# Whole runs of small TensorE tiles in a one-layer hybrid decoder step, with a planner that charges changes of tile shape

## The chip, the core and the metric

The kernel runs on one core of one Trainium2 chip. The metric is the device time of one execution in microseconds (us), as a median over runs. TensorE (PE in the profile) does the matrix products, VectorE (DVE) and ScalarE (ACT) the elementwise work, GpSimd (POOL) a little copying, and the queue of SyncE (SP) issues all DMAs. Each engine executes its own instructions in the order in which they stand in the program, and waits on semaphores for the others.

## What is computed

One layer of a decoder step, for a prompt of 512 tokens and for 8 samples of 4 tokens each. All tokens go through one input projection; branch A is dilated sliding-window attention with 3 groups of 8 heads, branch B a gated delta rule in chunks with 8 heads of 128; both are merged, projected and normed.

```python
h = x * (1 + scale[:, None]) + shift[:, None]
qa, ka, va, za, qkv_b, zb, a_b, b_b, ga, gb = split_columns(h @ w_in)       # 1024 x 11280
# branch A, for each group (window, dilation) in ((128,1),(512,4),(2048,16))
logits = einsum('bqhd,bqjhd->bqhj', q, k_sel) * 64 ** -0.5 + bias
p = exp(logits - max); s = sum(p); out = einsum('bqhj,bqjhd->bqhd', p / s, v_sel); lse = m + log(s)
o_a = combine over groups with softmax(lse)
# branch B, for each chunk
lower = where(strict, beta * kk * decay, 0) + eye(n)
sol = triangular_solve(lower, concat([beta * v, beta * k * exp(cum)]))       # u, w
v_new = u - w @ state; out = (q * exp(cum)) @ state + (qk * decay) @ v_new
state = exp(cum[-1]) * state + (k * tail).T @ v_new
# back
merged = sigmoid(ga) * ((o_a * silu(za)) @ w_branch_a) + sigmoid(gb) * ((norm(o_b) * silu(zb)) @ w_branch_b)
y = LayerNorm(ALPHA * x + gate * (merged @ w_out))
```

## The kernel before

**The stream.** The 544 token columns (512 prompt, 32 sample) stand in two halves of 272. The projection is cut into 88 jobs of one 128-column tile of `w_in` each. A job is 48 matmuls: for each half and each of 8 pieces of the contraction, three products of rounded halves (`hhi,hi`, `hhi,lo`, `hlo,hi`, all fp32r, 128x272) are summed into one PSUM bank `pp`, of which there are two. ScalarE and VectorE split each weight tile into `hi` and `lo` and empty the banks. Jobs of the branch outputs (`ybh`, `yah`) and the last product (`wo`) have the same manner. These matmuls fill TensorE wherever nothing else is ready.

**Side work.** Beside the stream run, as generators: the delta rule (`delta_blocks`, `delta_rule`, one head after the other), the prompt attention (`prompt_attention`, four head pairs j), and the samples. In the profile's names `pg<-k,q` is a score product of the prompt attention, `pg<-PT,vrow` a product with the values, `pg<-cst,P` a transpose between them, `pg<-cst,st` the transposes of the softmax sums at the end of two pairs, `pd<-Tc,NTs`, `pd<-W,Xc`, `pd<-XF,W`, `pd<-W,XF`, `pd<-U,NTs` and `pd<-XF,U` the stages of the triangular inverse, and `pd<-vn,kr`, `pd<-vn,QKd`, `pd<-S,KQ`, `pd<-z,XF` the steps of the delta rule over its four chunks.

**Shapes and positions.** A product whose contraction or whose output rows are under 128 uses a part of the TensorE array only: a score product takes 64 rows by 128 columns of it, a value product 128 by 64, an inverse stage 32 by 32 or 64 by 64. Score products of the two heads of a pair (`hh`) lie at array rows 0 and 64 and write two different banks; value products of the two heads lie at array columns 0 and 64 and write one bank `pn`. In the code the two heads alternate already. The 16 steps (j, i) of the attention have 6 score products each (two of them 256 columns wide where i is not 0) and 8 value products (6 where i is 0). Three PSUM banks (`pg`) serve scores, transposes and value sums together.

**The order.** Nothing is issued as it is written. A `Recorder` (line 245) notes every operation; `schedule` (line 419) then plays all engines on costs of its own (`cost`, line 335) and at each point gives an engine the ready operation of least rank (the stream has rank 9, the attention 3). The order that comes out is emitted for each engine. On PE it keeps two kinds apart, fp32r (`rounded`) and the rest: while fp32r is running, others that have been ready for less than `HOLD` = 1 us are kept back (line 551), and a change between the kinds is charged 0.054 or 0.097 us (line 576). Operations recorded under `together()` (line 328) form a group that is issued without another instruction of that engine between them. Before the change that is used for the sample values, the gate rows and a loop on VectorE, not for scores, prompt values or inverse stages. A new PSUM tile is given out when its first operation is a candidate.

**The end of the prompt attention.** After the last `st` transposes of the pairs j = 2 and 3 come VectorE's work on the weights `R` and `Z`, four DMAs `dw<-R` to device memory, eight DMAs `wv<-dw` back, and VectorE's products of `ya` and `NB` with them. The SBUF pools of that phase are then closed and those of the next opened, in which the first `zt` tile of the jobs `zb` lies. Two halves of a job can go to the two `pp` banks before that; the next half has to wait until `zt` has emptied one.

**The caches.** 168 DMAs of 512 KB (`out_kv_s<-in_cache`) copy the caches from device memory to device memory. Each has an earliest time in the planner's clock (48 to 850 us, evenly), so that they lie between the other DMAs of SP's queue.

Of the kernel before, what the change touches and what calls it, by code (L numbers as in the profile page):

```python
# [12 lines left out]
F32R = mybir.dt.float32r  # L13
# [230 lines left out]
class Recorder:  # L244
# [4 lines left out]
    OVER = {"ve": 0.08, "se": 0.10, "ge": 0.05}  # L249
    AGAIN = {"pe": 0.0, "ve": 0.11, "se": 0.14, "ge": 0.11, "sp": 0.0}  # L250
    HOLD = 1.0
    ENGINES = ("pe", "ve", "se", "ge", "sp")
    FREE = ("g", "d", "b")

# [72 lines left out]
    @contextmanager  # L327
    def together(self):

        self.group = []  # L330
        yield
        self.group = None


    def cost(self, op, args):
        size = lambda v: math.prod(v.shape[1:])
        views = op.outs + op.ins
        n = max([size(v) for v in views] or [1])
# [4 lines left out]
        op.transfer = None  # L343
        e = "sp" if op.name == "dma_start" else op.engine
        if e == "pe":
            op.rounded = False
            if op.name == "transpose":
                c = 0.117
            else:
                m, n = size(args[1]), size(args[2])  # L350
                op.rounded = args[1].dtype == F32R
                if op.rounded:
                    c = 0.455 * n + 2
                elif m > 64:
                    c = max(200, 1.93 * n + 5)
                elif m > 32:
                    c = max(120, 1.21 * n)
                else:
                    c = max(18, 0.57 * n)
                c /= 1000  # L360
            op.cost, op.late = c, 0.165
        elif e == "ve":
            if op.name == "reciprocal":
                c = 0.15 + 6.25e-3 * n
            elif op.name == "memset":
                c = 0.06 + 0.83e-3 * n
# [52 lines left out]
    def schedule(self):  # L419
# [33 lines left out]
        parked_pool, lanes, rounded = {}, {}, [True]  # L453
        busy, cold, held = [], {}, {}
        push, pop = heapq.heappush, heapq.heappop

        def candidate(op):
# [22 lines left out]
            for d, data in op.deps.items():  # L480
                p = ops[d]
                if p.engine != op.engine or p.transfer is not None:
                    r = max(r, p.done + self.WAKE[op.engine] + self.margin(p, op) if data else p.end)
                else:
                    r = max(r, p.end + (self.AGAIN[op.engine] if data else 0.0))
            for t in op.tiles:
# [30 lines left out]
        while done < len(ops):  # L517
# [28 lines left out]
            elif not avail[e]:  # L546
                free[e] = t
                continue
            else:
                op = None  # L550
                if e == "pe" and rounded[0] and not avail[e][0][-1].rounded:

                    if t - min(x[-1].ready for x in avail[e] if not x[-1].rounded) < self.HOLD:
                        x = min((x for x in avail[e] if x[-1].rounded), default=None)
# [153 lines left out]
def body(ctx, tc, io):  # L708
# [517 lines left out]
    def delta_rule(h):  # L1226
# [13 lines left out]
        for c in range(4):  # L1240
            for a in range(0, 128, 32):
                pe.matmul(pwv[a:a + 32, c, :], NTs[a:a + 32, c, a:a + 32], Tc[a:a + 32, c, 0:16],
                          start=True, stop=True, tile_position=(a, a))
# [4 lines left out]
        for c in range(4):  # L1248
            for a in range(0, 128, 32):
                pe.matmul(pxv[a:a + 32, c, :], Xc[a:a + 32, c, :], W0[a:a + 32, c, :],  # L1250
                          start=True, stop=True, tile_position=(a, a))
# [10 lines left out]
        for c in range(4):  # L1262
            for a in (0, 64):
                pe.matmul(pwv[a + 32:a + 64, c, :], NTs[a:a + 32, c, a + 32:a + 64], Tc[a:a + 32, c, :],
                          start=True, stop=True, tile_position=(a, a + 32))
# [5 lines left out]
        for c in range(4):  # L1271
            for a in (0, 64):
                x22 = XF[a + 32:a + 64, c, a + 32:a + 64]
                w = W[a + 32:a + 64, c, :]
                if a == 0:
                    pe.matmul(pxv[32:64, c, :], x22, w, start=True, stop=True, tile_position=(32, 32))
                pe.matmul(pxv[a:a + 32, c, :], w, x22, start=True, stop=True, tile_position=(a + 32, a))
# [4 lines left out]

        pw = pd()
        pwv = pw[:, 0:256].rearrange("p (s m) -> p s m", m=64)
        for c in range(4):
            pe.matmul(pwv[64:128, c, :], NTs[0:64, c, 64:128], U[0:64, c, :],
                      start=True, stop=True, tile_position=(0, 64))
# [4 lines left out]
        for c in range(4):  # L1292
            pe.matmul(pxv[0:64, c, :], U[64:128, c, :], XF[64:128, c, 64:128], start=True, stop=True,
                      tile_position=(64, 0))
        ve.tensor_scalar(XF[0:64, :, 64:128], pxv[0:64], -1.0, None, op0=OP.mult)
        yield 1.7

# [86 lines left out]
    def prompt_attention():  # L1384

        for j in range(4):
# [28 lines left out]
            def scores(i):  # L1415
# [1 line left out]
                tk = slice(128 * i, 128 * i + 128)  # L1417
                k0 = 0 if i else 128
                pS = [pg(), pg()]
                for g in range(3):  # L1420
                    for hh in range(2):
                        hp = slice(64 * hh, 64 * hh + 64)
                        if g == 0:
                            pe.matmul(pS[hh][:, k0:256], qt[0][hp, tk], kt[0][hp, 128 * (i - 1) + k0:128 * (i + 1)],
                                              start=True, stop=True)
                        else:
                            pe.matmul(pS[hh][:, 128 + 128 * g:256 + 128 * g], qt[g][hp, tk], kt[g][hp, tk],
                                      start=True, stop=True)
                Ps = []
                for hh in range(2):  # L1430
                    h4 = 2 * (j % 2) + hh
# [11 lines left out]
            for i in range(4):  # L1443
# [12 lines left out]
                    PTs.append(PT)  # L1456
                    yield 1.2 + 0.5 * hh

                for c in range(c0_, 4):
                    for hh in range(2):  # L1460
                        hp = slice(64 * hh, 64 * hh + 64)
                        g = max(c - 1, 0)
                        v = vrow[g][:, i - 1 if c == 0 else i, hp]
                        pe.matmul(pnv[hp, c > 1, i % 2, :], v, PTs[hh][:, c, :], start=c in (c0_, 2), stop=c in (1, 3))
# [812 lines left out]
```

## Time and profile before

| what | us |
|---|---|
| median of 3 runs (971.05 to 979.1) | 971.42 |
| span of the profiled execution, first to last instruction | 969.5 |
| PE busy / weight loads busy | 915.4 / 837.9 |
| DVE busy | 739.3 |
| ACT busy / POOL busy | 416.1 / 78.8 |

The profiled execution has no other time of its own than its span, which lies 1.9 us below the median; that difference holds what lies around the first and the last instruction, and the spread of the runs. All matmuls of one fp32 product (not of fp32r) stand as two records each, a product being done in two passes; a transpose is one record. Records of PE overlap, since matmuls are pipelined: the busy time of a group counts overlaps once, and the distance from one start to the next is what a matmul costs the stream. All operations carry the line of the helper that emits them (L655 before, L670 after), so groups are told apart by their tiles.

### The profile page before, as it was taken

The numbers are of one execution on the slowest core, as the hardware profiler recorded it, in microseconds if no ns is written. First come the engines' busy times: TensorE is split into PE (matmuls) and PEld (weight loads), VectorE is DVE, ScalarE is ACT, GpSimd is POOL, SyncE is SP. The second block draws the span as 40 slices with busy tenths as digits, with TensorE's granted clock in tenths as the row PEclk, the third lists the DMA queues.
The fourth block names the chain that finished last, engine by engine and source line by source line (L and its number), as shares of the span: only waits on it lengthen the run. The fifth ranks groups of instructions, "written<-read, shape, count | busy, mean of one in ns | idle before, by whom it ended". The sixth has DMA issues, their size and how long they took to land.

```text
span 969.5 us, 20678 instructions
## 1 busy us (share of the span) xinstructions
PE 915.4 (94%) x8070; PEld 837.9 (86%) x8070; DVE 739.3 (76%) x1620; ACT 416.1 (43%) x973; POOL 78.8 (8%) x176
## 2 busy tenths in 40 slices
PE   4899999999999999999999799998999999999895
PEld 1599988999988998889998698897998999997785
DVE  0575556866899999699989867556899899847658
ACT  0365347553657553457453546341532222234421
POOL 0110001100010300012402100002020000000000
PEclk9799999999999999999999799999999999999998
DMA  9677855676977697968787746559879999975513
GB/s 357 211 229 232 235 178 208 218 198 185 306 260 251 189 296 245 322 218 277 263 280 257 256 140 210 167 179 314 296 253 338 365 416 374 316 256 169 192 38 113
DMA packets 106340, 237.76 MB, mean 245 GB/s; under 512 B 30898, under 2 KB 62140, under 8 KB 103556
## 3 DMA queue, kind: packets, MB, share of 16 engines
q1 hardware_dynamic: 106244, 236.45, 72.7%
q8 instruction: 63, 1.03, 0.4%
q14 instruction: 33, 0.27, 0.1%
HBM read 220.40 MB, written 103.70 MB: 334 GB/s over the span
## 4 chain that ended last, share of the span: by engine, by line
PE 65%; DVE 18%; DMA 10%; issue 3%; ACT 2%; SPq 2%; POOL 0%; DVEq 0%; ACTq 0%; POOLq 0%
PE pp L655 48%; PE pg L655 9%; PE pd L655 5%; PE pb L655 3%; DVE lo L655 2%; DVE r L655 2%; DVE slab L655 2%; DMA wc<-in_w_cond 2%; DVE acc L655 2%; SPq L655 2%; DMA wv<-dw 1%; DMA out_kv_s<-in_cache 1%; DVE tmp L655 1%; DVE Tb L655 1%; DMA S<-in_state_delta 1%
## 5 line engine op out<-in xcount | busy, mean ns | idle before, releaser
L655 PE MATMUL pp<-hhi,hi 128*128 128x272 f32 x1408 | 414.5, 295 | 9.2 <-DVE zt L655 2.6
L655 PE MATMUL pp<-hhi,lo 128*128 128x272 f32 x1408 | 414.6, 295 | 0.0
L655 PE MATMUL pp<-hlo,hi 128*128 128x272 f32 x1408 | 411.9, 293 | 0.5 <-DVE hlo L655 0.5
L655 PEld LDWEIGHTS pp<-hhi,hi 128*128 128x128 f32 x1408 | 267.9, 190 | 12.9 <-DVE zt L655 3.0
L655 PEld LDWEIGHTS pp<-hlo,hi 128*128 128x128 f32 x1408 | 268.0, 190 | 3.1 <-issue 1.0
L655 PEld LDWEIGHTS pp<-hhi,lo 128*128 128x128 f32 x1408 | 267.5, 190 | 3.2 <-issue 2.2
L655 ACT ACTIVATE hi<-wt 128x1024 fp32r<-128x1024 f32 (+1 forms) x104 | 106.7, 1026 | 184.0 <-PE pp L655 148.7
L655 DVE TENSOR_TENSOR lo<-wt,hi 128x1024 fp32r<-128x1024 f32 (+1 forms) x104 | 122.6, 1179 | 58.1 <-ACT hi L655 55.5
L655 DVE SCALAR_TENSOR_TENSOR acc<-ext,cw,acc 128x568 f32<-128x568 f32 x72 | 57.5, 799 | 0.9 <-ACT acc L655 0.4
L655 ACT ACT_TABLE_LOAD x36 | 46.2, 1283 | 13.9 <-DMA cT<-in_cT 8.2
L655 DVE TENSOR_TENSOR slab<-slab 128x512 f32<-128x512 f32 (+1 forms) x66 | 42.8, 665 | 7.4 <-DMA slab<-in_vs 3.0
L655 ACT ACTIVATE P<-P,st 128x256 f32<-128x256 f32 (+1 forms) x64 | 31.3, 490 | 28.4 <-DVE st L655 27.9
L655 DVE TENSOR_REDUCE slab<-slab 128x8 f32<-128x512 f32 (+2 forms) x66 | 42.6, 655 | 0.3
L655 POOL COPY cx<-ext 128x3 f32<-128x3 f32 (+1 forms) x48 | 33.7, 732 | 75.2 <-ACT ext L655 75.0
L655 PE MATMUL pp<-ybh,hi 128*128 128x272 f32 x128 | 37.2, 290 | 1.3 <-ACT zt L655 1.3
L655 PE MATMUL pp<-ybl,hi 128*128 128x272 f32 x128 | 36.9, 289 | 0.0
L655 PE MATMUL pp<-ybh,lo 128*128 128x272 f32 x128 | 36.9, 288 | 0.0
L655 ACT ACTIVATE zt<-pp 128x272 f32<-128x272 f32 x48 | 18.5, 388 | 31.5 <-PE pp L655 31.5
L655 PE MATMUL pg<-k,q 64*128 64x128 f32 (+1 forms) x192 | 30.5, 329 | 0.0
L655 DVE CUSTOM_DVE_ANT_0 P<-pg,bias 128x256 f32<-128x256 f32 (+1 forms) x64 | 24.3, 402 | 6.2 <-PE pg L655 5.6
L655 ACT ACTIVATE ext<-pp 128x272 f32<-128x272 f32 (+2 forms) x72 | 20.0, 315 | 19.8 <-PE pp L655 16.4
L655 ACT ACTIVATE spare<-pp 128x272 f32<-128x272 f32 (+1 forms) x32 | 16.1, 503 | 26.0 <-PE pp L655 25.9
(395 smaller groups left out, 1587.0 us busy)
## 6 DMA issues: line engine op xcount, KB each, us to landing
out_kv_s<-in_cache SPq DMA_DIRECT2D x144, 512.0 KB
wt<-in_w_in SPq DMA_DIRECT2D x88, 512.0 KB
out_kv_s<-in_cache SPq DMA_DIRECT2D x24, 496.0 KB
wc<-in_w_cond SPq DMA_DIRECT2D x8, 1024.0 KB
slab<-in_ks SPq DMA_DIRECT2D x32, 256.0 KB
slab<-in_vs SPq DMA_DIRECT2D x32, 256.0 KB
kv<-in_ks SPq DMA_DIRECT2D x16, 512.0 KB
kv<-in_vs SPq DMA_DIRECT2D x16, 512.0 KB
```

Source lines behind the costliest of these rows:

```text
L655: getattr(real[x.engine], x.name)(*map(arg, x.args), **{k: arg(v) for k, v in x.kw.items()})
```

## The change

There are four parts. Six loops of the inverse stages, the score products and the value products are put under `together()`, with the operations unchanged. In a group each operation now depends in order on the one before it, and the first operation takes on all tiles of the group, so that the group begins only when all its banks are free and all its inputs are there. The planner's PE costs are changed: each product has a shape (`form`: rows and columns of the array, each 32, 64 or 128) and a `place` in it; a change of shape waits for all places and is charged `TURN` = 0.092 us; within a shape smaller than the whole array a product holds its own place for its cost and PE for `ISSUE` = 0.016 us; the costs are new (a transpose 0.111 for 0.117, an fp32 product with more than 64 output rows at least 0.222 us for 0.2, at 1.75 for 1.93 ns a column). And `HOLD` is kept per shape: while one shape is running, operations of another that have been ready for under 1 us are kept back.

```diff
         self.ops.append(op)
         if op.group is not None:
+            if op.group:
+                op.deps.setdefault(op.group[-1], False)
             op.group.append(op.n)
...
         self.group = []
         yield
+        first = self.ops[self.group[0]]
+        for n in self.group[1:]:
+            for t in self.ops[n].tiles:
+                if all(t is not x for x in first.tiles):
+                    first.tiles.append(t)
+                    if t.ops[0] in self.group:
+                        t.ops.insert(0, first.n)
         self.group = None
...
-                if op.rounded:
-                    c = 0.455 * n + 2
-                elif m > 64:
-                    c = max(200, 1.93 * n + 5)
-                elif m > 32:
-                    c = max(120, 1.21 * n)
-                else:
-                    c = max(18, 0.57 * n)
-                c /= 1000
+                c = max(0.222 if m > 64 else 0.116 if m > 32 else 0.06, 1.75e-3 * n)
...
-                if e == "pe" and rounded[0] and not avail[e][0][-1].rounded:
+                if e == "pe" and avail[e][0][-1].form != form:
...
             if e == "pe":
-                c += 0.0 if rounded[0] == op.rounded else 0.097 if op.rounded else 0.054
-                rounded[0] = op.rounded
+                if op.form != form:
+                    t = max([t] + list(places.values())) + self.TURN
+                    form, places = op.form, {}
+                elif form != (128, 128):
+                    t = max(t, places.get(op.place, 0.0))
...
+            if e == "pe" and form != (128, 128):
+                places[op.place] = op.end
+                free[e] = t + self.ISSUE
+            op.gone = free[e]
...
-                for g in range(3):
-                    for hh in range(2):
+                with rec.together():
+                    for g in range(3):
+                        for hh in range(2):
...
-                for c in range(c0_, 4):
-                    for hh in range(2):
+                with rec.together():
+                    for c in range(c0_, 4):
+                        for hh in range(2):
```

The inverse stages in `delta_rule` are wrapped in the same way (the loops over `c` and `a`).

The number of PE matmuls is the same. What moves is their order. The first place is on PE, in the first head pair (j = 0), where the values of one step and the scores of the next stand beside the delta rule. In these rows the last figure is the output's size and x the number of like instructions in a row. Before:

```order
L655 MATMUL pg<-PT,vrow 64x128
L655 MATMUL pg<-k,q 128x256
L655 MATMUL pd<-vn,kr 128x128
L655 MATMUL pd<-vn,QKd 128x128
L655 MATMUL pd<-S,KQ 128x128
L655 MATMUL pg<-PT,vrow 64x128 x7
L655 MATMUL pg<-k,q 128x256
L655 MATMUL pg<-k,q 128x128 x3
```

The same place now:

```order
L670 MATMUL pg<-PT,vrow 64x128 x8
L670 MATMUL pd<-vn,kr 128x128
L670 MATMUL pd<-vn,QKd 128x128
L670 MATMUL pd<-S,KQ 128x128
L670 MATMUL pg<-k,q 128x256 x2
L670 MATMUL pg<-k,q 128x128 x4
L670 MATMUL pd<-S,KQ 128x128
```

The eight value products and the six score products stand in one piece each, where they were split in two or more. Over the whole program the score products stood in 41 pieces and now stand in 16, one for each step; the value products stood in 32 and now stand in 16; the inverse stages stood in 49 pieces and stand in 48.

The second place is on PE at the end of the last pair (j = 3), where the `st` transposes end that VectorE waits for. Before:

```order
L655 MATMUL pg<-PT,vrow 64x128 x2
L655 MATMUL pg<-cst,st 4x128
L655 MATMUL pd<-vn,kr 128x128
L655 MATMUL pd<-vn,QKd 128x128
L655 MATMUL pg<-cst,st 4x128
L655 MATMUL pg<-cst,st 4x8x4 x16
L655 MATMUL pg<-cst,st 4x128 x2
L655 MATMUL pd<-S,KQ 128x128
L655 MATMUL pg<-cst,st 4x128 x2
L655 MATMUL pp<-hlo,hi 128x272
```

The same place now:

```order
L670 MATMUL pp<-hhi,hi 128x272
L670 MATMUL pg<-cst,st 4x8x4 x12
L670 MATMUL pg<-cst,st 4x128 x4
L670 MATMUL pd<-vn,kr 128x128
L670 MATMUL pd<-vn,QKd 128x128
L670 MATMUL pd<-S,KQ 128x128
L670 MATMUL pp<-hlo,hi 128x272
```

The last `st` transpose stands later against the stream. Counted in the order of PE, 3,084 matmuls into `pp` stand ahead of it before and 3,153 now. The products `pb<-kq`, which stand where PE has filled both `pp` banks for the next phase, have 3,248 matmuls into `pp` ahead of them in both.

The third place is on DVE, the products with the weights `wv` and what follows up to the first `zt` of the next phase. Before:

```order
L655 SCALAR_TENSOR_TENSOR spare<-spare,pp 128x272
L655 TENSOR_TENSOR ya<-ya,NB 128x512
L655 TENSOR_TENSOR lo<-wt,hi 128x1024
L655 SCALAR_TENSOR_TENSOR ya<-ya,spare 128x512
L655 TENSOR_TENSOR NB<-NB,wv 128x4x4x32
L655 TENSOR_TENSOR ya<-ya,NB 128x512
L655 SCALAR_TENSOR_TENSOR ya<-ya,spare 128x512
L655 SCALAR_TENSOR_TENSOR nd<-pb,beta,nd 128x128
L655 TENSOR_TENSOR lo<-wt,hi 128x1024
L655 SCALAR_TENSOR_TENSOR zt<-zt,pp 128x272 x2
```

The same place now:

```order
L670 TENSOR_TENSOR lo<-wt,hi 128x1024
L670 TENSOR_TENSOR ya<-ya,wv 128x4x4x32
L670 TENSOR_TENSOR NB<-NB,wv 128x4x4x32
L670 TENSOR_TENSOR ya<-ya,wv 128x4x4x32
L670 TENSOR_TENSOR ya<-ya,NB 128x512
L670 TENSOR_TENSOR NB<-NB,wv 128x4x4x32
L670 SCALAR_TENSOR_TENSOR ya<-ya,spare 128x512
L670 TENSOR_TENSOR ya<-ya,NB 128x512
L670 SCALAR_TENSOR_TENSOR ya<-ya,spare 128x512
L670 SCALAR_TENSOR_TENSOR zt<-zt,pp 128x272 x2
```

The two splits of weights (`lo`) that stood among these operations now stand ahead of them.

On SP 120 of the 168 cache copies stand ahead of the loads of the sample states (`S<-in_state_delta`) now, 126 before; after the last load of sample values (`kv<-in_vs`) follow 15 copies now, 10 before.

More of the change, by code (lines that the diff above doesn't have):

```diff
@@ L251 @@
     HOLD = 1.0
+    TURN, ISSUE = 0.092, 0.016
     ENGINES = ("pe", "ve", "se", "ge", "sp")
@@ L452, in schedule @@
         port, queue, table = {"ve": 0.0, "ge": 0.0}, {True: 0.0, False: 0.0}, None
-        parked_pool, lanes, rounded = {}, {}, [True]
+        parked_pool, lanes, form, places = {}, {}, (128, 128), {}
         busy, cold, held = [], {}, {}
@@ L483, in candidate @@
                     r = max(r, p.done + self.WAKE[op.engine] + self.margin(p, op) if data else p.end)
+                elif op.engine == "pe":
+                    r = max(r, p.gone)
                 else:
@@ L550, in schedule @@
                 op = None
-                if e == "pe" and rounded[0] and not avail[e][0][-1].rounded:
-                    if t - min(x[-1].ready for x in avail[e] if not x[-1].rounded) < self.HOLD:
-                        x = min((x for x in avail[e] if x[-1].rounded), default=None)
+                if e == "pe" and avail[e][0][-1].form != form:
+                    if t - min(x[-1].ready for x in avail[e] if x[-1].form != form) < self.HOLD:
+                        x = min((x for x in avail[e] if x[-1].form == form), default=None)
                         if x:
@@ L1239, in delta_rule @@
         pwv = pw[:, 0:64].rearrange("p (s m) -> p s m", m=16)
[L1240 to L1243, printed above, removed]
+        with rec.together():
+            for c in range(4):
+                for a in range(0, 128, 32):
+                    pe.matmul(pwv[a:a + 32, c, :], NTs[a:a + 32, c, a:a + 32], Tc[a:a + 32, c, 0:16],
+                              start=True, stop=True, tile_position=(a, a))
         ve.tensor_copy(W0, pwv)
@@ L1247, in delta_rule @@
         pxv = px[:, 0:64].rearrange("p (s m) -> p s m", m=16)
[L1248 to L1251, printed above, removed]
+        with rec.together():
+            for c in range(4):
+                for a in range(0, 128, 32):
+                    pe.matmul(pxv[a:a + 32, c, :], Xc[a:a + 32, c, :], W0[a:a + 32, c, :],
+                              start=True, stop=True, tile_position=(a, a))
         ve.scalar_tensor_tensor(Tc[:, :, 0:16], pxv, C("low16"), Tc[:, :, 0:16], op0=OP.mult, op1=OP.add)
@@ L1261, in delta_rule @@
         pwv = pw[:, 0:128].rearrange("p (s m) -> p s m", m=32)
[L1262 to L1265, printed above, removed]
+        with rec.together():
+            for c in range(4):
+                for a in (0, 64):
+                    pe.matmul(pwv[a + 32:a + 64, c, :], NTs[a:a + 32, c, a + 32:a + 64], Tc[a:a + 32, c, :],
+                              start=True, stop=True, tile_position=(a, a + 32))
         for a in (32, 96):
@@ L1270, in delta_rule @@
         pxv = px[:, 0:128].rearrange("p (s m) -> p s m", m=32)
[L1271 to L1277, printed above, removed]
+        with rec.together():
+            for c in range(4):
+                for a in (0, 64):
+                    x22 = XF[a + 32:a + 64, c, a + 32:a + 64]
+                    w = W[a + 32:a + 64, c, :]
+                    if a == 0:
+                        pe.matmul(pxv[32:64, c, :], x22, w, start=True, stop=True, tile_position=(32, 32))
+                    pe.matmul(pxv[a:a + 32, c, :], w, x22, start=True, stop=True, tile_position=(a + 32, a))
         se.activation(U[32:64, :, 0:32], pxv[32:64], AF.Copy, scale=-1.0)
@@ L1284, in delta_rule @@
         pwv = pw[:, 0:256].rearrange("p (s m) -> p s m", m=64)
-        for c in range(4):
-            pe.matmul(pwv[64:128, c, :], NTs[0:64, c, 64:128], U[0:64, c, :],
-                      start=True, stop=True, tile_position=(0, 64))
+        with rec.together():
+            for c in range(4):
+                pe.matmul(pwv[64:128, c, :], NTs[0:64, c, 64:128], U[0:64, c, :],
+                          start=True, stop=True, tile_position=(0, 64))
         ve.tensor_copy(U[64:128], pwv[64:128])
@@ L1291, in delta_rule @@
         pxv = px[:, 0:256].rearrange("p (s m) -> p s m", m=64)
-        for c in range(4):
-            pe.matmul(pxv[0:64, c, :], U[64:128, c, :], XF[64:128, c, 64:128], start=True, stop=True,
-                      tile_position=(64, 0))
+        with rec.together():
+            for c in range(4):
+                pe.matmul(pxv[0:64, c, :], U[64:128, c, :], XF[64:128, c, 64:128], start=True, stop=True,
+                          tile_position=(64, 0))
         ve.tensor_scalar(XF[0:64, :, 64:128], pxv[0:64], -1.0, None, op0=OP.mult)
@@ L1419, in scores @@
                 pS = [pg(), pg()]
-                for g in range(3):
-                    for hh in range(2):
[L1422 to L1428, printed above, removed]
+                with rec.together():
+                    for g in range(3):
+                        for hh in range(2):
+                            hp = slice(64 * hh, 64 * hh + 64)
+                            if g == 0:
+                                pe.matmul(pS[hh][:, k0:256], qt[0][hp, tk], kt[0][hp, 128 * (i - 1) + k0:128 * (i + 1)],
+                                          start=True, stop=True)
+                            else:
+                                pe.matmul(pS[hh][:, 128 + 128 * g:256 + 128 * g], qt[g][hp, tk], kt[g][hp, tk],
+                                          start=True, stop=True)
                 Ps = []
@@ L1457, in prompt_attention @@
                     yield 1.2 + 0.5 * hh
-                for c in range(c0_, 4):
-                    for hh in range(2):
[L1461 to L1464, printed above, removed]
+                with rec.together():
+                    for c in range(c0_, 4):
+                        for hh in range(2):
+                            hp = slice(64 * hh, 64 * hh + 64)
+                            g = max(c - 1, 0)
+                            v = vrow[g][:, i - 1 if c == 0 else i, hp]
+                            pe.matmul(pnv[hp, c > 1, i % 2, :], v, PTs[hh][:, c, :], start=c in (c0_, 2), stop=c in (1, 3))
                 if i % 2:
```

12 lines of the change are left out of this document (8 added, 4 removed).

## The prediction

> **What bounds the kernel now.** I read the page first, then the idle time of PE, then the stretches. A view by cores says nothing more for one core.
>
> ```profile
> span 969.5 us, 20678 instructions
> ...
> PE 915.4 (94%) x8070; PEld 837.9 (86%) x8070; DVE 739.3 (76%) x1620; ACT 416.1 (43%) x973; POOL 78.8 (8%) x176
> ...
> PE   4899999999999999999999799998999999999895
> ...
> DVE  0575556866899999699989867556899899847658
> ```
>
> PE is busy in nearly every slice, DVE too in the middle. A busy PE is not yet a PE at its best, since its records overlap: what counts is the distance of starts. The stretches say where there is slack.
>
> ```profile
> 250.00:550.00 300.00, 286.95 (x2705) 263.62 (x2703) 273.51 (x667) 155.79 (x398) 39.46 (x78) 0.99 0.79 262
> 550.00:650.00 100.00, 98.75 (x1007) 90.41 (x1008) 63.97 (x184) 47.87 (x131) 4.92 (x14) 0.97 0.55 175
> 650.00:700.00 50.00, 44.49 (x518) 39.93 (x517) 37.40 (x65) 18.41 (x32) 8.78 (x12) 1.00 0.92 298
> 700.00:850.00 150.00, 147.22 (x1214) 143.34 (x1213) 136.60 (x170) 41.21 (x74) 5.37 (x7) 1.00 0.94 346
> 850.00:907.00 57.00, 56.75 (x410) 48.13 (x408) 34.87 (x64) 22.37 (x41) 0.00 (x0) 1.00 0.63 208
> ```
>
> The columns after the length are PE, weight loads, DVE, ACT and POOL busy, the granted clock and the DMA share. From 250 to 550 PE is idle for 13 us and DVE for 26.5; from 550 to 650 PE for 1.3. So PE's own work sets the time up to the end of the attention, with DVE close behind in the middle. From 650 to 700 PE is idle for 5.5 us, and the chain of waits tells why.
>
> ```profile
> 631.61 0.70 DVE R L655
> ...
> 640.41 2.31 DMA dw<-R
> ...
> 645.26 5.38 DMA wv<-dw
> ...
> 659.82 0.44 DVE zt L655
> ```
>
> ```profile
> 653.81 0.40 PE L655 MATMUL pp<-hhi,hi 128*128 128x272 f32 x1 [1.36 <-DVE spare L655]
> ...
> 660.30 0.39 PE L655 MATMUL pp<-hhi,hi 128*128 128x272 f32 x1 [2.36 <-DVE zt L655]
> ```
>
> When the last pair of heads has its softmax sums, a chain of 660.30 - 631.61 = 28.7 us runs over DVE, two round trips of DMAs and DVE again; PE has stream work for 25 us of it and stands for 3.7. This chain matters below.
>
> **The score products.** What an uninterrupted piece costs, and a split one, can be read in the same trace (start, length, what; two records a product):
>
> ```profile
> 258.93 0.39 PE L655 MATMUL pd<-vn,QKd 128*128 128x128 f32 x2
> 259.16 0.39 PE L655 MATMUL pd<-S,KQ 128*128 128x128 f32 x2
> 259.47 0.94 PE L655 MATMUL pg<-k,q 64*128 64x128 f32 x12
> 260.34 0.39 PE L655 MATMUL pp<-hlo,hi 128*128 128x272 f32 x1
> ...
> 268.45 1.15 PE L655 MATMUL pg<-k,q 64*128 64x256 f32 x12
> ...
> 138.83 0.49 PE L655 MATMUL pd<-S,KQ 128*128 128x128 f32 x2
> 139.25 0.49 PE L655 MATMUL pg<-k,q 64*128 64x128 f32 x2
> 139.66 0.39 PE L655 MATMUL pp<-hhi,lo 128*128 128x272 f32 x1
> ```
>
> Six products that alternate between the two positions take 0.94 us, a single one 0.49: within a piece the two positions work at once, alone each pays a start and an end. Where i is not 0, two of the six are 256 wide and the piece takes 1.15. The groups as they are now, and two pieces of value products:
>
> ```profile
> L655 PE MATMUL pg<-k,q 64*128 64x128 f32 (+1 forms) x192 | 30.5, 329 | 0.0
> L655 PE MATMUL pg<-PT,vrow 128*64 128x128 f32 x240 | 22.3, 284 | 0.1
> ```
>
> ```profile
> 135.51 0.88 PE L655 MATMUL pg<-PT,vrow 128*64 128x128 f32 x12
> ...
> 162.48 0.28 PE L655 MATMUL pp<-hhi,lo 128*128 128x272 f32 x1
> 162.69 1.12 PE L655 MATMUL pg<-PT,vrow 128*64 128x128 f32 x16
> 163.74 0.39 PE L655 MATMUL pp<-hhi,hi 128*128 128x272 f32 x1
> ```
>
> The order now has 16 whole pieces: 4 x 0.94 + 12 x 1.15 = 17.6 us for 30.5, a gain of 12.9.
>
> **The value products.** 16 whole pieces: 4 x 0.88 + 12 x 1.12 = 17.0 us for 22.3, a gain of 5.3. The Trainium skill (TensorE: Matmul & The Clock Gate, Part 3, The mechanism) speaks against it: weight loads overlap running matmuls only where the array rows differ, and these two positions share all rows. The trace does not bear it out: eight products start within 163.74 - 162.69 = 1.05 us with the change of shape in it, 0.13 each, where a whole-array product of the same width needs 259.16 - 258.93 = 0.23.
>
> **The changes of shape.** Ahead of the scores S,KQ holds PE for 259.47 - 259.16 = 0.31 us instead of 0.23, so entering a shape costs about 0.08 to 0.09. A piece's busy time already counts 0.07 that overlaps what follows (0.94 against 260.34 - 259.47 = 0.87), so the 25 + 16 = 41 pieces fewer give only some 0.02 each beyond the sums, 0.8. PE's gain: 12.9 + 5.3 + 0.8 = 19.0 us, all of it before the last `st` transpose.
>
> **The inverse stages.** Already whole, 49 pieces for 48 now:
>
> ```profile
> 266.50 0.44 PE L655 MATMUL pd<-W,Xc 32*32 32x16 f32 x32
> ```
>
> All 16 products of a stage lie in one piece of 0.44 us. I take 0 (bounds -0.3 and +0.3, a change of shape either way at three places).
>
> **What the later `st` costs.** Three starts of the stream, beside the value piece above, and the two splits of weights that stood within the last part of the chain:
>
> ```profile
> 162.10 0.29 PE L655 MATMUL pp<-hhi,lo 128*128 128x272 f32 x1
> 162.23 0.29 PE L655 MATMUL pp<-hhi,hi 128*128 128x272 f32 x1
> 162.35 0.29 PE L655 MATMUL pp<-hlo,hi 128*128 128x272 f32 x1
> ...
> 654.28 1.22 DVE L655 TENSOR_TENSOR lo<-wt,hi 128x1024 fp32r<-128x1024 f32 x1
> ...
> 658.69 1.22 DVE L655 TENSOR_TENSOR lo<-wt,hi 128x1024 fp32r<-128x1024 f32 x1
> ```
>
> From 162.10 to 162.48 it is three starts, 0.127 us a matmul. The last `st` transpose has 69 more of them ahead of it, 8.8 us. So the start of the chain comes 19.0 - 8.8 = 10.2 us earlier, not 19.0, and the work that covers it up to `pb<-kq` shrinks from 164 matmuls to 95. The chain itself changes a little: the two splits now stand ahead of its last part, 2.4 us at most; on SP all eight `wv` DMAs now go out in a row behind one more DMA of the delta rule, so I take 1.4 (bounds 0 and 2.4). PE resumes 10.2 + 1.4 = 11.6 us earlier, and stands for some 10 us instead of 3.7.
>
> **The rest.** Behind the boundary the order is much the same; the sample chain is a little later against the stream, which only lengthens its cover. SP has six cache copies moved from before the state loads to after them, five of them behind the last load of sample values, where the DMA share is 0.63 (850 to 907).
>
> ```profile
> q1 hardware_dynamic: 106244, 236.45, 72.7%
> ```
>
> 236.45 MB took 0.727 x 969.5 = 705 us, so a copy of 0.5 MB is about 1.6 us and five are 8, in a stretch with 0.37 x 57 = 21 us free: 0 (if that cover went, 8). The other terms are the clock and the waits that the new order makes or loses.
>
> ```profile
> PE pd L655 <- DVE z L655: 3.4, 2, 3.0
> ```
>
> ```profile
> 500.00:550.00 50.00, 43.41 (x427) 39.37 (x425) 44.92 (x106) 20.32 (x41) 6.65 (x10) 0.96 0.79 258
> 550.00:600.00 50.00, 48.75 (x463) 45.44 (x464) 34.00 (x106) 27.99 (x77) 3.41 (x10) 0.94 0.59 189
> ```
>
> In these two stretches the granted clock fell to 0.96 and 0.94, so 50 x 0.04 + 50 x 0.06 = 5 us of clock were lost, in the half in which PE waited 3.0 us in one piece. The Trainium skill (TensorE: Matmul & The Clock Gate, Part 1) has it that an idle window of about 3.4 us halves the clock until a busy one; by that the longer stand at the boundary loses clock too. From the rows the bounds are 0 and +5 for the new stand and 0 and -8 (3 + 5) for the old wait, if the new order has it no more; I take 0 for both together.
>
> **Sum.** On the profiled execution 969.5 - 11.6 = 957.9; the median of the runs lies 1.9 above its span, so 959.8, I say 960.
>
> **Rivals.** (1) *The forecast*, 0.52: PE gives 19 us and the boundary takes over 7 of them; 960, own range 954 to 967. (2) *The boundary does not bind*, 0.20: the attention of the last pair is reached with waits saved elsewhere, or the chain is shorter than today's. For it: PE stands only 3.7 us there now, and the old 3.0 us wait may go. Against: 28.7 us of chain with 95 matmuls (12 us) of stream ahead of the stop. The whole gain arrives: 971.4 - 19 = 952. (3) *DVE becomes the bound in the middle*, 0.19: half of the gain (j = 1, 2) lies from 250 to 550, where 273.5 us of DVE stand in 300 and would stand in 290, 94%; each late DVE operation then stops PE, as engines go in order. Half of 19 is lost again: 960 + 9 = 969. (4) *Slower*, 0.06: a whole piece is issued only when all its inputs and two of the three banks are there, and if they come later than the planner thought, PE stands in front of it with all the stream behind; a split piece could begin with one bank. There are 32 such places; at 0.4 us each the 11.6 are gone, and at 0.7 us (22 us) the time passes 981. Against: scores and values show 0.0 and 0.1 us of idle in the groups above. At 0.8 us, 32 x 0.8 = 26, the time is 971.4 - 11.6 + 26 = 986. (5) *Value pieces do not overlap*, 0.03, the rule above as a mechanism: 120 products x 0.23 = 27.6 us for 22.3, so PE gains 19.0 - 5.3 - 5.3 = 8.4, less 8.8 at the boundary, plus 1.4: 970. That the change does not do what it says has no chance of its own: the order shows the pieces whole.
>
> **Numbers.** About 1% (9.7 us) is what a measurement of this kernel can tell from no change, so faster means under 961.7. Of (1) six tenths lie there, 0.31, and all of (2), 0.20: faster 0.51. Slower is (4), 0.06. The rest, 0.43, is within 1%. The range 950 to 971 takes in (1), (2), (3) and (5) but for their ends.
>
> **What would show it.** Scores busy near 17.6 us (30.5 now) and values near 17.0 (22.3) show the first two steps; values over 24 would show the rule right. The `zt` wait of PE at the boundary should grow to about 10 us, with the last `st` near 621 us and PE going on near 649. If PE goes on near 641, (2) holds; if PE's idle time from 250 to 550 grows well past 13 us, (3); if waits show in front of `pg<-k,q` or `pg<-PT,vrow`, (4). I am wrong altogether if the pieces stand whole and their busy time does not fall.

## The result and the profile after

The changed kernel takes 940.18 us (939.77 to 940.85), the kernel before 971.52 in the same comparison: a ratio of 0.9653, with a 95% interval of 0.9618 to 0.9689. It is 31 us faster; 11.6 were forecast, and the time lies below the whole range of the forecast, 950 to 971. The page of the profiled execution after:

```profile
span 938.0 us, 20669 instructions
...
PE 892.0 (95%) x8070; PEld 825.8 (88%) x8070; DVE 736.8 (79%) x1620; ACT 417.0 (44%) x975; POOL 64.0 (7%) x176
...
PE   4799999999999999999999998988999999999995
...
DVE  1575556876799999889989997556899789957768
```

PE's busy time fell by 23.4 us, its idle time (span less busy) by 8, from 54.1 to 46.0. The two groups that the forecast spoke of, in the list of the costliest groups:

```profile
L670 PE MATMUL pg<-k,q 64*128 64x128 f32 (+1 forms) x192 | 17.5, 315 | 0.0
L670 PE MATMUL pg<-PT,vrow 128*64 128x128 f32 x240 | 16.9, 279 | 0.0
```

Scores went from 30.5 to 17.5, values from 22.3 to 16.9. The stretches, with the columns of before (PE, weight loads, DVE, ACT, POOL busy, granted clock, DMA share):

```profile
250.00:550.00 300.00, 295.89 (x2966) 279.15 (x2965) 280.60 (x683) 169.69 (x437) 30.33 (x84) 1.00 0.77 259
550.00:600.00 50.00, 46.89 (x499) 42.62 (x498) 42.02 (x133) 25.04 (x69) 2.45 (x5) 0.97 0.67 226
600.00:650.00 50.00, 41.01 (x424) 36.78 (x426) 25.36 (x48) 15.10 (x32) 4.01 (x10) 0.90 0.69 225
700.00:850.00 150.00, 150.00 (x1251) 146.84 (x1250) 131.18 (x164) 42.43 (x73) 0.00 (x0) 1.00 0.95 355
```

From 250 to 550 PE is idle for 4.1 us where it was 13.1, and from 700 to 850 for none where it was 2.8. DVE, busy for 273.5 us of the 300 before, now is for 280.6, and PE waits less all the same. Two stretches got worse. From 550 to 600 PE is idle for 3.1 us where it was 1.3, in one wait for DVE ahead of products of the samples:

```profile
578.80 0.64 PE L670 MATMUL pg<-slab 96*32 96x256 f32 x8 [3.07 <-DVE st L670]
```

More was lost at the end of the attention, now between 600 and 650: PE is idle there for 9.0 us, where it was for 5.5 between 650 and 700. There, DVE's copy of the weights `R`, the chain of waits, and PE's next matmul:

```profile
614.88 0.69 DVE L670 COPY R<-pg 128x512 f32<-128x512 f32 x1
```

```profile
625.59 4.85 DMA wv<-dw
630.54 0.98 DVE ya L670
...
637.04 0.36 DVE zt L670
```

```profile
637.44 0.59 PE L670 MATMUL pp<-hhi,hi 128*128 128x272 f32 x1 [8.75 <-DVE zt L670]
```

PE stands for 8.75 us there, where 2.36 and 1.36 were. The forecast's marks were: stand about 10, and PE going on near 649. It goes on at 637.4.

### The profile page after: what moved, and what is told of

Read it like the earlier page. It is cut to its first block, busy times and chain, and to the rows that moved or that the text cites. A ratio compares the mean times of both kernels' runs of the same rounds, so it can differ in the third digit from the quotient of the medians.

```text
span 938.0 us, 20669 instructions
## 1 busy us (share of the span) xinstructions
PE 892.0 (95%) x8070; PEld 825.8 (88%) x8070; DVE 736.8 (79%) x1620; ACT 417.0 (44%) x975; POOL 64.0 (7%) x176
## 4 chain that ended last, share of the span: by engine, by line
PE 72%; DVE 11%; DMA 4%; ACT 3%; issue 2%; SPq 0%; POOL 0%; DVEq 0%; POOLq 0%; ACTq 0%
PE pp L670 55%; PE pg L670 7%; PE pd L670 6%; PE pb L670 3%; DVE slab L670 2%; DMA dO<-orow 1%; DMA wv<-dw 1%; DMA slab<-in_vs 1%; DVE lo L670 1%; ACT L670 1%; DVE XF L670 1%; DVE r L670 1%; ACT hi L670 1%; DVE ya L670 1%; DVE acc L670 0%
## 5 line engine op out<-in xcount | busy, mean ns | idle before, releaser
L670 ACT ACTIVATE P<-P,st 128x256 f32<-128x256 f32 (+1 forms) x64 | 31.3, 491 | 19.7 <-DVE st L670 19.5
L670 POOL COPY cx<-ext 128x3 f32<-128x3 f32 (+1 forms) x48 | 23.3, 515 | 94.0 <-ACT ext L670 93.9
L670 ACT ACTIVATE vn<-pd,beta 128x128 f32<-128x128 f32 x32 | 11.7, 366 | 34.4 <-PE pd L670 34.3
L670 DVE TENSOR_TENSOR Tb<-Tb,tmp 32x15 f32<-32x15 f32 (+7 forms) x120 | 23.4, 195 | 4.1
L670 PE MATMUL pp<-wc,cs 128*32 128x512 f32 x64 | 13.1, 916 | 14.3 <-DMA wc<-in_w_cond 14.3
L670 ACT ACTIVATE ext<-pp 128x272 f32<-128x272 f32 (+2 forms) x72 | 20.0, 314 | 14.9 <-PE pp L670 13.9
```

Source lines behind the costliest of these rows:

```text
L670: getattr(real[x.engine], x.name)(*map(arg, x.args), **{k: arg(v) for k, v in x.kw.items()})
```

## The experiments

All of them have the products of the kernel before; they differ in the order only. For each I took three sums from its trace and its planner. **Work**: over all products on PE, in the order of that kernel, the median distance to the next start that the same product with the same kind of neighbours (same shape and position, other position, other shape) has in the trace of before; given as the difference to before. **Waits**: the real distances less these medians, so PE's standing and lost clock (16 to 19 of them, in the first 50 us, in all kernels alike). **Overcharge**: the PE time that the planner reckoned for the order, without its planned waits for data, less the same medians. The planner also charges for a slow clock, 8 to 16 us in these orders; that charge is in the overcharge, while the clock really lost is in the waits.

| kernel | time, us | ratio to before | work | waits | of these ahead of scores | overcharge |
|---|---|---|---|---|---|---|
| before | 971.5 | 1 | 0 | 60.4 | 0.3 | 24.9 |
| changed | 940.2 | 0.965 | -20.3 | 49.3 | -0.1 | 12.0 |
| e1 groups only | 976.6 | 1.002 | -20.0 | 84.1 | 11.9 | 47.3 |
| e2 new numbers only | 952.5 | 0.978 | -5.3 | 47.0 | 1.2 | 4.0 |
| e3 old hold rule | 935.5 | 0.961 | -20.0 | 44.6 | 0.0 | 9.0 |
| e4 no charge for shapes | 934.3 | 0.960 | -20.0 | 44.5 | -0.1 | -14.9 |
| e5 e1 + score price | 953.7 | 0.981 | -19.4 | 61.6 | 0.2 | 29.7 |
| e6 scores planned serially | 951.1 | 0.977 | -19.7 | 62.1 | 5.6 | 21.5 |
| e7 before + whole-array price | 967.7 | 0.994 | 0.0 | 56.8 | 1.7 | 15.6 |
| e8 e1 + whole-array price | 952.3 | 0.979 | -19.0 | 60.1 | 5.4 | 30.1 |
| e9 e1 + later reads | 968.7 | 0.995 | -19.4 | 74.5 | 0.7 | 47.7 |
| e10 e1 + both prices | 941.2 | 0.966 | -20.6 | 50.5 | -0.2 | 22.5 |
| e11 e3 and e4 together | 939.0 | 0.964 | -21.0 | 49.6 | 0.7 | -12.1 |
| e12 no inverse groups | 936.6 | 0.962 | -21.5 | 46.1 | 0.0 | 7.3 |
| e13 changed, old whole-array price | 937.6 | 0.962 | -19.3 | 46.2 | 0.8 | 14.6 |
| e14 changed, low whole-array price | 937.5 | 0.962 | -20.6 | 45.3 | 0.7 | 2.0 |
| e15 changed again | 940.2 | 0.965 | -20.3 | 49.9 | -0.1 | 12.0 |
| e16 e4 again | 934.4 | 0.958 | -20.0 | 44.4 | -0.2 | -14.9 |

Ratios go by runs of the kernel before on the same chip; their 95% intervals reach 0.002 to 0.004 to either side. Work and waits add up: e1 has 20.0 less work and 23.7 more waits, and its span is 973.0 for 969.5.

### Groups or numbers

e1 is the kernel before with the new `together()`, the eight groups, and nothing of the planner's numbers. e2 is the changed kernel with its eight groups taken out:

```diff
# e1, on the kernel before, in add(), and at the eight loops
+            if op.group:
+                op.deps.setdefault(op.group[-1], False)
...
+        with rec.together():
# e2, on the changed kernel, at the eight loops
-        with rec.together():
+        if True:
```

> The kernel before with the eight uninterrupted groups (scores, values, six inverse stages) and nothing of the new numbers: costs, hold rule and charges of the planner as before. Scores and values stand in 16 whole pieces each, so PE has the same work as after the change: 20.0 us less than before, summed with the distances of starts in the trace of before. The change gained 31.3 us, 11 more than that. Theory W (the whole pieces themselves also take the waits of the middle away): 940 +-4, PE idle between 250 and 550 us near 4 us as after the change. Theory N (the planner's new numbers take the waits away, by an order that fits the chip better): the work alone, less what the boundary of the phases takes, so 952 to 962, PE idle from 250 to 550 near 13 us as before. Theory D (which waits remain is a matter of chance in each order): anywhere from 940 to 962.

> The changed kernel without its eight new groups: the planner has the new costs, charges and hold rule, and may split pieces. Scores stand in 34 pieces (41 before, 16 after), values in 30 (32, 16); PE has 5.3 us less work than before by the same sum of distances. Theory W: 971.5 - 5.3 = 966 +-4, with the waits of the middle as before. Theory N: the 11 us of waits go here too, 971.5 - 5.3 - 11 = 955 +-4, PE idle from 250 to 550 near 4 us. Theory D: anywhere from 950 to 968.

e1 gained nothing, with pieces as whole as in the changed kernel; e2, with 34 and 30 pieces, gained 21 us. Theory W falls on both counts. e2 lies where theory N put it, with PE idle for 7.8 us from 250 to 550, not near 4. e1 lies outside all three ranges, with PE idle there for 18.9 us: none of the theories had the groups make new waits. The work is saved in e1 too, but it turned into waits: 11.9 us ahead of score products (8.0 of them stand as idle time in the group below), 6.9 at `pd<-S,KQ`, and the clock. The waits by line, and the group:

```profile
PE pg L664 <- DVE st L664: 8.8, 15, 1.3
```

```profile
L664 PE MATMUL pg<-k,q 64*128 64x128 f32 (+1 forms) x192 | 22.6, 329 | 8.0 <-DVE st L664 8.0
```

```profile
550.00:600.00 50.00, 46.40 (x431) 43.11 (x430) 30.99 (x76) 26.93 (x77) 2.58 (x10) 0.89 0.60 178
```

That is close to the fourth rival, waits at whole score pieces, but in the kernel that lacks the other half of the change. One piece shows what PE waits for. First PE, then DVE:

```profile
432.30 0.49 PE L664 MATMUL pd<-S,KQ 128*128 128x128 f32 x2
432.72 0.70 PE L664 MATMUL pg<-k,q 64*128 64x256 f32 x4
434.71 0.71 PE L664 MATMUL pg<-k,q 64*128 64x128 f32 x8 [1.28 <-DVE st L664]
```

```profile
433.16 0.69 DVE L664 TENSOR_TENSOR slab<-slab 128x512 f32<-128x512 f32 x1 [0.38 <-DMA slab<-in_vs]
...
434.24 0.40 DVE L664 CUSTOM_DVE_ANT_0 P<-pg,bias 128x256 f32<-128x256 f32 x1
434.57 0.08 DVE L664 DVE_READ_ACCUMULATOR2_ANT st<- 128x1 f32 x1
```

The stand is inside the piece. After its first two products (256 columns each, one for each bank) PE stops until DVE has read those columns for the softmax, and then does the other four. The planner had reckoned the two products at 0.5 us each, one after the other (426.29 to 427.28 on its clock). DVE's read thus came out at 427.21, in the order ahead of the third product at 427.28. On the chip the two products are done in 0.70, while DVE comes to the read late, behind other work. The planner reckons no wait here: its test whether another engine has the bank (`turn` in `schedule`) is not made for products of a group that has begun. The program that is emitted does make PE wait for the read. The Trainium skill (PSUM — Partial Sum Buffer, PSUM bank collisions raise a hardware error) has it that two engines may not touch the same quadrant of a bank at once, other columns included, and that a dependency is put between them; this trace shows such a dependency, with 1.28 us of PE waiting for a read of other columns. What the chip would do without it no run here shows. In nine of the sixteen pieces of e1 such a read stands among the products in the planner's order, so 11.9 / 9 = 1.3 us a piece on average. In the changed kernel none does:

```profile
428.00 1.15 PE L670 MATMUL pg<-k,q 64*128 64x256 f32 x12
429.08 0.39 PE L670 MATMUL pp<-hhi,hi 128*128 128x272 f32 x1
```

```profile
429.18 0.42 DVE L670 CUSTOM_DVE_ANT_0 P<-pg,bias 128x256 f32<-128x256 f32 x1
```

### The hold rule and the charge for shapes

e3 puts the old test back, which holds products back by rounded or not; e4 sets the charge to nothing:

```diff
# e3
-                if e == "pe" and avail[e][0][-1].form != form:
+                if e == "pe" and rounded[0] and not avail[e][0][-1].rounded:
# e4
-    TURN, ISSUE = 0.092, 0.016
+    TURN, ISSUE = 0.0, 0.016
```

> The changed kernel with the old hold rule (a product that isn't rounded may wait up to 1 us while rounded ones are ready, instead of any product of another shape). Same pieces, same PE work within 0.3 us. W and N: 940 +-3, since neither rests on this rule. D: a different order with different waits, over 4 us from 940 on either side.

> The changed kernel with the planner's charge for a change of shape at 0 instead of 0.092 us; the groups keep all pieces whole, and PE has the same work within 0.3 us. The planner's PE is now some 237 x 0.092 = 22 us too fast, so its due times run ahead of the chip, as they did before the change. Theory N: waits come back, 946 to 955, PE idle from 250 to 550 back near 10 us or more. Theory W: 940 +-4. Theory D: anywhere from 936 to 955.

Neither lost anything: e4 is somewhat faster than the changed kernel (e15 and e16 below compare the two on one chip), and e3 is not clearly so, with 0.961 for 0.965. Neither the hold rule nor the charge, from which the change has its name, is a source of the gain. e3 lies 4.5 us under 940, where only theory D put it, and e4 lies under all three ranges. That e4 lost nothing also corrects theory N: its planner takes PE for 15 us faster than the medians, and no waits came of that.

### Which number: the score price

e5 halves the price of a score product in e1, and e6 takes the overlap of the two positions out of the changed planner for scores alone:

```diff
+                if m > 64 and args[1].shape[0] == 64:
+                    c /= 2
```

```diff
-            if e == "pe" and form != (128, 128):
+            if e == "pe" and form not in ((128, 128), (64, 128)):
```

> The kernel with the groups alone, and one more edit: the planner's price of a score product is halved (0.126 us for 128 columns). With the old price the planner took 16 whole score pieces for 30.1 us of PE, where they need 17.6. Theory S (an overpriced piece is the cause: the planner fills the time beside the softmax with too little stream, and PE stands in front of the score products for what was charged too much): the waits ahead of score products, 11.9 us in all with the groups alone, fall under 3, and the time falls by 12 to 20 from that kernel's, to 950-962. Theory F (the price of whole-array products, 0.252 us planned and 0.222 to 0.23 on the chip, is the cause): within 5 us of the groups alone, the waits move elsewhere.

> The changed kernel, except that the planner takes the score products one after another (0.222 us each, no overlap of the two positions), so it plans 16 pieces for some 26 us in place of 15; the pieces stay whole. Theory S: 8 to 12 us of waits ahead of score products come back and the time rises to 946-953. Theory F: 940 +-4 as after the change, no waits ahead of score products.

Both times came out as theory S has it, and so did the waits in e5; in e6 5.6 us of waits came back ahead of score products, where 8 to 12 were expected. The group in e5, and in e6:

```profile
L666 PE MATMUL pg<-k,q 64*128 64x128 f32 (+1 forms) x192 | 17.5, 315 | 0.0
```

```profile
L670 PE MATMUL pg<-k,q 64*128 64x128 f32 (+1 forms) x192 | 20.5, 323 | 3.6 <-DVE st L670 3.6
```

By the ratios the price alone takes 21 us off e1, and planning the score products one after another costs the changed kernel 11. The way it works is not the one that theory S names, though. In e6 four of the sixteen pieces have a read inside, for 5.6 us; in e5 none. e9 tests that by itself: e1 with its old prices, and each read made to depend on the last product of its piece:

```diff
+                last = rec.ops[-1].n
...
+                        rec.ops[-1].deps[last] = True
```

> The kernel with the groups alone and all old numbers, and one dependence more: the four softmax reads of a score piece on VectorE may only be placed behind the last product of that piece. With the groups alone nine of the sixteen pieces have such a read of their own bank among their products in the program's order, and PE then stands inside the piece. Theory B (that order is what costs; the price matters since it decides whether a read fits in between): waits ahead of score products fall from 11.9 to under 2, and the time by 8 to 14, to 963-969. Theory L (the overpriced piece as such costs, since too little other work is planned beside the softmax chain): the waits turn up at the next products, time within 5 of the groups alone, 972-980.

```profile
L664 PE MATMUL pg<-k,q 64*128 64x128 f32 (+1 forms) x192 | 18.2, 316 | 0.3 <-DVE PT L664 0.3
```

The waits ahead of score products fell from 11.9 to 0.7 and the time by about 7 us against before (1.002 to 0.995). So the reads inside the pieces are what made PE stand at the scores, and theory B is right there. But 14 of e1's 24 extra us of waits stayed at other products, so it is not the whole of what the old prices cost: the halved price, which also leaves no read inside a piece, gained three times as much. What makes PE stand at the other products stays open.

### The other price

e7 sets the new price of whole-array products in the kernel before, e8 sets it in e1:

```diff
-                    c = max(200, 1.93 * n + 5)
+                    c = max(222, 1.75 * n)
...
-                c = 0.117
+                c = 0.111
```

> The kernel before, no groups, with the new price of unrounded whole-array products (0.222 us or 1.75 ns a column in place of 0.252 at 128 columns) and of transposes (0.111 for 0.117), and nothing else. PE has the same work as before within 0.1 us (39 score pieces for 41). Theory S: 971 +-4. Theory F: this price is what took the waits away in the kernel with the new numbers alone, so 12 to 16 us faster, 955-960.

> The groups alone, with the new price of whole-array products and transposes, the old price of score products. Theory S: waits ahead of score products stay near 10 us, time within 6 us of the groups alone (968-980). Theory F: the waits fall to those of the changed kernel, 945-955. If both prices matter, between the two, near 960.

This edit does more than the expectations say. A score product has over 64 output rows too, so its price falls as well, from 0.252 to 0.224 us at 128 columns; e7 and e8 do not test whole-array products alone. In e7 the edit gave 0.6%, half of what theory F asks for. In e8 it took 23 us off e1: the time lies in theory F's range, but the waits, 60.1, did not fall to the 49.3 of the changed kernel. e8 still has 5.4 us ahead of scores, with a read inside five pieces where e1 has nine. e10 has both prices:

> The groups with both prices corrected (half price of a score product, 0.222 for a whole-array product, 0.111 for a transpose), and none of the rest of the new numbers: no charge per shape, no positions, old hold rule. If the two prices are what the change needed: 938-945. If the rest is needed as well: 948-954, no better than with one price.

941.2 us: the groups and two prices are the whole result, without the charge for shapes, positions or the new hold rule (the old charge for a change of kind is still in it). But the second price is not needed when the rest of the new numbers is there:

> The changed kernel with the old price of whole-array products and transposes alone put back (0.252 us at 128 columns, 0.117). If a price above the chip's makes PE stand, whichever product it belongs to: 947-954, as with the groups and the score price alone. If the rest of the new numbers makes up for it: 937-943.

> The changed kernel with whole-array products priced as far below the new price as the old one was above it (0.192 us at 128 columns). If what costs is any distance from the chip's time: 947-954. If only a price above the chip's costs, since PE then comes earlier than planned and stands, while with a price below it comes later and finds all there: 934-942.

```diff
# e13
-                c = 0.111
+                c = 0.117
...
+ ... if op.form != (128, 128) else max(0.2, 1.93e-3 * n + 0.005)
# e14
+ ... if op.form != (128, 128) else max(0.192, 1.51e-3 * n)
```

They take 937.6 and 937.5, e14 with a price as far below the new one as the old one lay above it. These two do change whole-array products alone. What goes with the waits in the table is the sum rather than one price. The eight different kernels with an overcharge under 15 us have 44 to 50 us of waits, down to an overcharge of -15. Of the eight above that, five (15.6 to 30.1) have 57 to 62, and the two at 47 have 75 and 84; e10, with 22.5, has 50.5 and is the exception. The border is not sharp: without the planner's charge for a slow clock e7 lies at 2.5 us and e13 at 4.9, with 56.8 and 46.2 us of waits. Nor are prices and rules well separated, for seven of the eight above have the old rules of the planner and all eight below the new ones (e3 and e11 but for the hold rule); only e6, above with the new rules, and e10, with the old rules and few waits, speak for the prices. So my reading is that a planner that takes PE to be slower than it is makes PE stand, since the products of other engines come at the planned time and PE ahead of it, and that one that takes it to be faster does not. This is not shown as a rule; shown step by step it is only for the score pieces.

### The rest

e11 joins the edits of e3 and e4; e12 takes the groups (`together()`, as in e2) from the six inverse loops alone.

> The changed kernel with the old hold rule and no charge for a change of shape, which each alone gave 935.5 and 934.3 for 940.2. If these were effects of their own, they add: 929-931. If they were the scatter of one order against another: 932-941.

> The changed kernel without the six groups of the inverse stages; the planner keeps them whole but for one by itself. The forecast put them at 0: 940 +-4, the scatter of one order against another. If the groups help beyond that: 945 or more; if they do harm by holding PE for 16 products: 935 or less.

e11 does not add the two gains, so the hold rule and the charge have no effects of their own that these runs could tell from a changed order. e12 is no slower without the inverse groups.

e15 is the changed kernel, e16 that of e4, both with no other edit.

> The changed kernel once more, beside the others of this call on one chip: 940 +-2, for a direct comparison with the two above and the one below.

> The changed kernel without the planner's charge for a change of shape once more, which gave 934.3 on another chip: if it is faster than the changed kernel, 934 +-2 with that at 940; if chips made the difference, both alike within 2.

On one chip the changed kernel takes 938.8 to 944.1 us and the one without the charge 933.5 to 937.2. That is 0.6%, and the fastest kernel here. It has less work ahead of the last softmax sums, 3,056 matmuls of the stream for 3,153, and stands for 0.20 us only at the end of the attention, where the changed kernel stands for 8.75:

```profile
628.77 0.40 PE L670 MATMUL pp<-hhi,hi 128*128 128x272 f32 x1 [0.20 <-DVE spare L670]
```

I take this for a lucky order rather than a rule, since e11 shares the charge of 0 and lies at 939.0.

## Why the prediction was wrong

**Scores and values** were right: 17.6 and 17.0 us forecast, 17.5 and 16.9 measured, and the sum of distances gives 20.3 us less work for the forecast's 19.0. The fifth rival, values that do not overlap, put them at 27.6 and falls. The rule beside it in the Trainium skill (TensorE: Matmul & The Clock Gate, Part 3, The mechanism) is that weight loads overlap running products only on other array rows; the 16.9 us of these two column positions do not bear out the time that was worked out with it. Why a value product is cheap is not separated here: the two positions may work at once, but its weight load is also shorter, with a mean of 136 ns for 194 at `pd<-S,KQ` in the kernel before, and no run has one position alone. **Inverse stages** at 0: e12 bears it out.

**The end of the attention** was right in kind. It takes over a part of the gain, with a stand of 8.75 us for about 10. The chain itself was mis-sized: from `R` to PE's next matmul it takes 637.44 - 614.88 = 22.6 us for 28.7, 6.1 less where 1.4 was put, beyond the bound of 2.4. From `R` to the last wait for `wv` it is 3.5 shorter, and behind that DVE has fewer other operations in the row, 2.7 shorter; only the two splits of weights (2.4) had been seen.

**The rest, put at 0, is the step that failed.** The start of the chain, `R`, comes 16.7 us earlier than before, not 10.2: ahead of it waits and lost clock went too (the idle time from 250 to 550 is 8.9 us less, and the clock from 550 to 600 is 0.97 for 0.94). Behind the boundary, which was put as "much the same", the kernel needs 938.0 - 637.4 = 300.6 us for 969.5 - 660.3 = 309.2, 8.6 less. So the miss is 6.5 + 4.7 + 8.6 = 19.8 us, and 11.6 + 19.8 = 31.4 is the difference of the spans, 31.5, but for rounding. The bound of -8 for clock and waits was taken from one wait of 3 us and its clock; it left out that an order planned with other prices has other waits everywhere. That the long stand goes with a lower clock, for which up to 5 us were allowed, did come: 0.90 from 600 to 650.

The reason behind it: the forecast read the change as whole pieces and worked out what they save. It went through the planner's new costs only for the order that they give. By the runs, the whole pieces without the new costs are worth nothing (e1). That is in part because the old prices place DVE's reads inside them, which is worth about 7 us (e9); the rest of e1's waits stays open. The new costs with few whole pieces are worth 21 us (e2), and by the table 13 us of that is waits and clock that no count of pieces shows. Only on top of the new costs do the whole pieces gain, 12 us from e2 to the changed kernel. The fourth rival named the waits at whole pieces and was given 0.06 on the ground that score products show 0.0 us of idle before. That reading was of split pieces: eleven of the sixteen had a read of DVE among their products before, too, but in most of them other products stand beside the read, and PE did those meanwhile.

## What to carry to other kernels

Where an order is planned on costs, a group that cannot be interrupted makes a wrong price expensive: whatever another engine does on the group's own banks must not be placed inside it, and here a price too high is what let it in. When prices change, compare the planner's time for each kind of product with the distances in the trace, kind by kind; here too high a price for PE mostly went with PE standing, too low a price with nothing. And forecast a re-planned order with a range that admits that waits go or come all over the kernel: eight orders with the same work to within 2.2 us (the changed kernel, e3, e4 and e10 to e14) spread over 934 to 941 us, and the five others with about that work (e1, e5, e6, e8, e9) over 951 to 977.

## What was not expected of the hardware

A read of one half of a PSUM bank by DVE holds up PE's writes to the other half, although no byte is shared: 1.3 us a piece on average in nine pieces of e1. It is the program's semaphore that PE waits for there; what the chip itself would do is not shown.

A stand in the middle can cost twice, though not each time. In e1 the granted clock from 550 to 600 us was 0.89, where before had 0.94 and e2 1.00, so up to 5.5 us of the 50 were lost there, a part of them while PE stood anyway. But from 650 to 700 in the kernel before, PE was idle for 5.5 us at a clock of 1.00.
